# First stage of a decoder-layer kernel: conditioning sums gathered by a selection matrix, x transposed by token blocks, weight splits and parameter transposes reordered, separate waits for the next pool

## The chip, the cores and the metric

The kernel runs on one core of a Trainium2 chip. The time is device microseconds (us) of one execution on that core; the median over the runs is compared. Engines are called PE (TensorE, matmuls; its weight loads are shown apart as PEld), DVE (VectorE), ACT (ScalarE), POOL (GpSimd) and SP (SyncE, which here only issues DMAs).

## The reference

One inference step of a hybrid decoder layer: 512 prompt tokens and 8 sample tokens, width 1024. The part that the change touches is the start: the modulation from the conditioning vectors `c` (1 prompt, 8 samples), the first normalisation, and the first products with `w_in`.

```python
cs = jax.nn.silu(c.astype(F32))
mod = cs @ w_mod[l].astype(F32) + b_mod[l].astype(F32)        # 1024 -> 6*1024
sh1, sc1, g1, sh2, sc2, g2 = [m[:, None, :] for m in jnp.split(mod, 6, axis=-1)]
h = _rmsnorm(x, norm1_g[l]) * (1.0 + sc1) + sh1
u = h @ w_in[l].astype(F32)                                   # 1024 -> 8*1024
...                                                           # HGRN2, RG-LRU, two branches, w_out
x = (x.astype(F32) + g1 * (merged @ w_out[l].astype(F32))).astype(dt)
h2 = _rmsnorm(x, norm2_g[l]) * (1.0 + sc2) + sh2
ff = jnp.square(jax.nn.relu(h2 @ w_ff1[l].astype(F32))) @ w_ff2[l].astype(F32)
x = (x.astype(F32) + g2 * ff).astype(dt)
```

## The kernel before

All activations lie transposed: 128 features on the partitions, 520 tokens (512 + 8) along the row, in 8 blocks `k` of features. A large product (`products`, recorded at L111) takes fp32 data split into a high part in fp32r and a low part; each block `k` has 6 matmuls over halves of 260 columns: `whi` with h's high part, `whi` with h's low part, `wlo` with h's high part. Weights arrive by DMA in tiles `wst` of 512 KB; ACT casts the high part (`whi`), DVE subtracts it (`wlo`).

The first stage goes like this.

- SP issues the loads of c, x, the modulation weights `wm` (two tiles of 1 MB, scale and shift, for each pair of blocks k = 0, 2, 4, 6) and the first `wst` tiles. POOL issues the small parameter rows (`rb`, `rc`, `rd` among them).
- `transposed` turns x by PE transposes (L444) into the 4 banks of `pmm`, two blocks k at a time, and ACT and DVE copy the banks out (L445). `norm_x` and `normed` make the reciprocal root for each token; DVE multiplies (L459) all 8 blocks into `u`, which shares its memory with x as loaded (`xn`, so that name stands for u in the rows).
- `mod(k)` (L364) multiplies the conditioning, as a 32-column stationary operand `cT` of which 9 columns are used, by the two `wm` tiles. Four accumulations run side by side in the four 32-partition groups of one PSUM bank `ps` (j = 0 the first 256 columns, j = 1 the other 256): so four partial sums are left on partitions 0-31, 32-63, 64-95 and 96-127. ACT copies the bank to `modev` (L367).
- `mod_close` transposes modev in 4 pieces (L379), DVE adds the four partial sums with two reductions (L384), the bias (L387) and multiplies by the norm's gain (L391): `modT`.
- `affine_split(k)` makes h for blocks k and k+1: the sample columns on DVE (L468, L469), the high part on ACT (L472, with a cast of the sample columns, L476), the same in fp32 on DVE (L477) and the low part as the difference (L478).
- Between these, PE runs the products of the blocks that are ready, into two accumulators `acc` (the `pmm` banks), for the first two W_in tiles; `self.turn` chains the order on PE, `self.last_hi` and `self.split_last` that on ACT and DVE (`behind(a, b)`: a stands behind b).
- `parameters_in` transposes the small parameters (L224, rows rb, rc, rd, rd into `ps`) and DVE copies them (L225: pa, pb, pc). Then the pool `start`, which held the stage's memory, is closed and the pool `hg` opened in its place. The third W_in tile comes next, into the bank of the first sums once ACT has read them (L139, `e` and `X`).

`ps` has two PSUM banks (`pps`), used in turn; `pt` and `pb` have one each. What stands in a row on each engine is set by a scheduler within these chains; each engine then works its row in order. Later in the kernel, `mod_quarter` uses `mod` and `mod_close` for the other four parts, 8 times, each with one weight tile (so j = 0 alone, 512 columns).

The selection matrix of the change stands in the kernel already: `mdiag`, 128 x 4 x 32, is 1 where the partition modulo 32 equals the column:

```python
nc.vector.tensor_scalar(pi, pi, 31, None, OP.bitwise_and)
nc.vector.tensor_tensor(x, pi, ti, OP.bitwise_xor)
self.mdiag = sb.tile([128, NC, 32], F32, name="mdiag")
nc.vector.tensor_scalar(self.mdiag, x, 0.0, None, OP.is_equal)
```

Of the kernel before, what the change touches and what calls it, by code (L numbers as in the profile page):

```python
# [6 lines left out]
F32 = mybir.dt.float32  # L7
# [4 lines left out]
OP = mybir.AluOpType  # L12
# [4 lines left out]
L = 512  # L17
# [3 lines left out]
KO = D // 128  # L21
# [29 lines left out]
class Kernel:  # L51
# [304 lines left out]
    def mod(self, ws, ev, place):  # L356
# [3 lines left out]
        for j, w in enumerate(ws):  # L360
            n = w.shape[2]
            for k in range(KO):
                r = 32 * (k % 4)
                ins = nc.tensor.matmul(ps[r:r + 32, j * n:j * n + n], self.cT[:, k, :], w[:, k, :], start=k < 4, stop=k >= KO - 4)  # L364
                if self.ppt_free:
                    self.turn = self.behind(ins, self.turn) if self.turn else ins
        ins = nc.scalar.copy(ev, ps)  # L367
        if self.ppt_free and self.last_hi:
            self.behind(ins, self.last_hi)
        self.mod_open = ev, place  # L370

    def mod_close(self, after):
# [5 lines left out]
        for j in range(4):  # L378
            after = self.behind(nc.tensor.transpose(pt[:, j * 128:(j + 1) * 128], ev[:, j * 128:(j + 1) * 128], self.ident), after)  # L379
        out = self.modT.rearrange("p (a k) b -> p a k b", k=KO)[:, p0:p0 + np, k0:k0 + nk]  # L380
        bias = self.bmod.rearrange("p (a k) -> p a k", k=KO)[:, p0:p0 + np, k0:k0 + nk]
        got = pt.rearrange("p (a k j b) -> p a k b j", a=np, k=nk, b=32)[:, :, :, :NM]
        for a in range(np):
            ins = nc.vector.tensor_reduce(out[:, a], got[:, a], mybir.AxisListType.X, OP.add)  # L384
            if self.ppt_free and self.split_last:
                self.behind(ins, self.split_last)
        nc.vector.tensor_tensor(out, out, bias[..., None].to_broadcast([128, np, nk, NM]), OP.add)  # L387
# [43 lines left out]
    def transposed(self):  # L431
# [8 lines left out]
        for k in range(0, KO, 2):  # L440
            ps = self.pmm.tile([128, 2, 512], F32, name="mm")
            for j in range(2):
                for t in range(NC):
                    nc.tensor.transpose(ps[:, j, t * 128:(t + 1) * 128], self.xn[:, t, (k + j) * 128:(k + j + 1) * 128], self.ident)  # L444
                (nc.vector.tensor_copy if j else nc.scalar.copy)(self.x[k + j][:, :L], ps[:, j])  # L445

    def normed(self):
# [10 lines left out]
        for k in range(KO):  # L458
            nc.vector.tensor_tensor(self.u[:, k], self.x[k], rsb, OP.mult)  # L459

    def affine_split(self, k0):
# [7 lines left out]
        nc.vector.tensor_tensor(f[:, :, L:], f[:, :, L:], sh[:, :, 1:9], OP.add)  # L469
# [1111 lines left out]
```

## Time and profile before

| | us |
|---|---|
| median of 3 runs (lowest, highest) | 1018.2 (1018.13, 1018.38) |
| the profiled execution | 1018.91 |
| its span (first to last instruction) | 1017.1 |
| PE busy | 982.7 (97%) |
| DVE busy | 692.5 (68%) |
| ACT busy | 515.3 (51%) |
| the first stage, until the third W_in tile starts on PE | 52.42 |

The span is what the profiler sees from the first instruction to the last; the execution's time has some 1.8 us around it. A row of the timeline gives start, duration, engine, line and operation, output <- inputs with their shapes, how many instructions it groups, and in brackets the idle time of the engine before it with what released it. "PE busy" is modelled from pipelined matmuls. The granted clock is 1.00 at full speed.

### The profile page before, as it was taken

The numbers are of one execution on the slowest core, as the hardware profiler recorded it, in microseconds if no ns is written. First come the engines' busy times: TensorE is split into PE (matmuls) and PEld (weight loads), VectorE is DVE, ScalarE is ACT, GpSimd is POOL, SyncE is SP. The second block draws the span as 40 slices with busy tenths as digits, with TensorE's granted clock in tenths as the row PEclk, the third lists the DMA queues.
The fourth block names the chain that finished last, engine by engine and source line by source line (L and its number), as shares of the span: only waits on it lengthen the run. The fifth ranks groups of instructions, "written<-read, shape, count | busy, mean of one in ns | idle before, by whom it ended". The sixth has DMA issues, their size and how long they took to land.

```text
span 1017.1 us, 23291 instructions
## 1 busy us (share of the span) xinstructions
PE 982.7 (97%) x9585; PEld 955.5 (94%) x9585; DVE 692.5 (68%) x1543; ACT 515.3 (51%) x985; POOL 106.8 (10%) x193
## 2 busy tenths in 40 slices
PE   4999999999999999999999999999999999999995
PEld 3799999999999999999998999999999999999994
DVE  7678697687878868473233348667766776768775
ACT  5445753574565356351122234466556645646653
POOL 3000000000000000120000000022321331232040
PEclk9899999999999999999999999999999999999998
DMA  9884354344344434496656755322762483283242
GB/s 298 253 264 112 103 150 138 102 141 127 111 119 128 116 96 127 147 294 212 194 187 196 241 166 148 102 84 53 157 166 69 110 191 89 62 181 71 64 83 85
DMA packets 212572, 145.78 MB, mean 143 GB/s; under 512 B 6262, under 2 KB 196878, under 8 KB 212458
## 3 DMA queue, kind: packets, MB, share of 16 engines
q1 hardware_dynamic: 202562, 132.37, 43.9%
q0 software_dynamic: 9904, 11.92, 6.3%
q8 instruction: 75, 1.23, 0.5%
q14 instruction: 31, 0.25, 0.1%
HBM read 123.61 MB, written 13.39 MB: 135 GB/s over the span
## 4 chain that ended last, share of the span: by engine, by line
PE 88%; ACT 5%; DVE 4%; DMA 2%; issue 1%; SPq 0%; DVEq 0%; ACTq 0%
PE mm L111 63%; PE ps L1118 8%; PE pt L1118 4%; PE ps L364 2%; PE pb L1118 2%; PE pb L746 1%; PE ps L610 1%; DMA wst<-in_w_ff_dram 1%; DMA xn<-in_x_prompt_dram 1%; PE pt L677 1%; PE mm L1118 1%; PE pt L688 1%; PE pt L690 1%; ACT L794 1%; ACT L787 1%
## 5 line engine op out<-in xcount | busy, mean ns | idle before, releaser
L111 PE MATMUL mm<-h,whi 128*128 128x260 f32 (+1 forms) x3072 | 509.4, 285 | 1.9 <-ACT X L139 1.2
L111 PEld LDWEIGHTS mm<-h,whi 128*128 128x128 f32 x3072 | 426.9, 189 | 6.6 <-issue 4.1
L111 PE MATMUL mm<-h,wlo 128*128 128x260 f32 (+1 forms) x1536 | 313.1, 284 | 1.8 <-DVE wlo L80 1.4
L77 ACT CAST whi<-wst 128x1024 fp32r<-128x1024 f32 x166 | 173.6, 1049 | 218.0 <-PE mm L111 164.2
L80 DVE TENSOR_TENSOR wlo<-wst,whi 128x1024 fp32r<-128x1024 f32 x166 | 202.6, 1221 | 92.6 <-ACT whi L77 91.3
L111 PEld LDWEIGHTS mm<-h,wlo 128*128 128x128 f32 x1536 | 239.4, 189 | 2.3 <-DVE wlo L80 1.5
L111 PE MATMUL mm<-a,whi 128*128 128x260 f32 x512 | 83.0, 283 | 1.1 <-DVE rst L878 1.1
L111 PEld LDWEIGHTS mm<-a,whi 128*128 128x128 f32 x512 | 70.3, 188 | 2.1 <-issue 2.1
L111 PE MATMUL mm<-a,wlo 128*128 128x260 f32 x256 | 51.9, 283 | 0.0
L1214 DVE TENSOR_TENSOR f<-f 128x260 f32<-128x260 f32 x64 | 27.3, 427 | 28.9 <-ACT f L1209 28.2
L847 POOL DMA_DIRECT2D t<-oaT_d x8 | 4.3, 551 | 380.6 <-DVE wlo L80 374.7
L1203 ACT ACTIVATE ft<-ft,fsh 128x512 f32<-128x512 f32 (+2 forms) x36 | 24.0, 676 | 35.9 <-DVE ft L1200 35.9
L111 PE MATMUL mm<-b,whi 128*128 128x260 f32 x256 | 41.6, 284 | 0.0
L1206 POOL TENSOR_TENSOR ft<-ft,fsh 128x8 f32<-128x8 f32 x28 | 18.5, 659 | 216.9 <-DVE ft L1200 216.9
L111 PEld LDWEIGHTS mm<-a,wlo 128*128 128x128 f32 x256 | 39.4, 188 | 0.0
L111 PEld LDWEIGHTS mm<-b,whi 128*128 128x128 f32 x256 | 35.0, 188 | 2.5 <-ACT t L139 2.5
L596 DVE TENSOR_TENSOR Y<-Y,tb 128x512 f32<-128x512 f32 x40 | 27.5, 688 | 8.3 <-PE ps L610 7.2
L1248 POOL DMA_DIRECT2D ma<-snap x28 | 27.4, 979 | 35.4 <-issue 23.0
L863 DVE TENSOR_TENSOR t<-mm,t 128x520 f32<-128x520 f32 x8 | 5.6, 700 | 37.0 <-PE mm L111 37.0
L1230 POOL DMA_DIRECT2D ma<-snap x28 | 26.1, 932 | 43.8 <-DMA ma<-snap 27.2
L1209 ACT ACTIVATE f<-ft 128x520 f32<-128x520 f32 (+1 forms) x36 | 20.8, 587 | 14.9 <-POOL ft L1207 12.9
L555 ACT ACTIVATE st<-st,fkq 128x128 f32<-128x128 f32 x64 | 19.6, 389 | 16.4 <-DVE fkq L535 12.3
(488 smaller groups left out, 1815.0 us busy)
## 6 DMA issues: line engine op xcount, KB each, us to landing
wst<-in_w_in_dram SPq DMA_DIRECT2D x64, 512.0 KB, 4.3
wm<-in_w_mod_dram SPq DMA_DIRECT2D x8, 2048.0 KB, 7.9
wst<-in_w_ff_dram SPq DMA_DIRECT2D x64, 256.0 KB, 4.1
wst<-in_w_ff_dram SPq DMA_DIRECT2D x32, 512.0 KB, 4.0
wm<-in_w_mod_dram SPq DMA_DIRECT2D x8, 1024.0 KB, 10.7
st<-in_state_hgrn_dram SPq DMA_DIRECT2D x8, 512.0 KB, 4.9
vb<-vd SPq DMA_DIRECT2D x8, 512.0 KB, 4.0
out_dram<-st SPq DMA_DIRECT2D x8, 512.0 KB, 3.2
```

Of the source, the lines that this page charges most:

```text
L77: ins = self.nc.scalar.copy(hi, st)
L80: ins = self.nc.vector.tensor_tensor(lo, st, hi.bitcast(F32), OP.subtract)
L111: self.last_product = self.nc.tensor.matmul(ps[:, s, :c.stop - c.start], x, y[:, c], start=first and n == 0, stop=last and n == 2)
L364: ins = nc.tensor.matmul(ps[r:r + 32, j * n:j * n + n], self.cT[:, k, :], w[:, k, :], start=k < 4, stop=k >= KO - 4)
L555: nc.scalar.activation(st[:, b], st[:, b], AF.Copy, scale=fkq[:, 0, b:b + 1])
L596: made = nc.vector.tensor_tensor(view(Y, b, 0, 2 * b, n, b), view(X, b, 0, 2 * b, n, b), fac, OP.mult)
L1118: ins = self.nc.tensor.matmul(ps, x[:, w], y[:, f], start=j in (1, 7, 2) and k == 0 and n == 0, stop=k == 3 and n == 2, skip_group_check=True)
L1203: nc.scalar.activation(t[:, :p], t[:, :p], AF.Relu, bias=sh[:, 0:1])
L1209: nc.scalar.activation(f, self.two(self.ft)[:, a:a + n], AF.Square)
L1214: self.nc.vector.tensor_tensor(f[:, n], f[:, a], f[:, b], op)
L1230: nc.gpsimd.dma_start(x[1][:, b], v[:, :n], accum_op=OP.add)
L1248: nc.gpsimd.dma_start(x[t][:, a], s[p], accum_op=OP.add)
```

## The change

1. `mod` copies each half of the bank (j = 0, j = 1) with a copy of its own.
2. `mod_close` multiplies each 128-column piece of modev by the first 9 columns of `mdiag` instead of transposing it: the product adds the four partial sums and turns them at once, in 36 columns of `pt`. One DVE add with the bias (L385) takes the place of two reductions and an add.
3. `transposed` goes over token blocks first, and writes into 8 banks (the four of `pmm`, `pb`, both `ps`, `pt`); the 8 copies follow at the end, 5 on ACT and 3 on DVE.
4. `normed` no longer multiplies all 8 blocks at once: `scaled(n)` is called for blocks 0 to 3 before mod(0) and 4 to 7 before mod(2), each time behind the split of one weight tile. In `affine_split` the two blocks go one after the other on DVE.
5. `parameters_in` stands behind `affine_split(2)` instead of behind the last products.
6. The pool `hg` is opened with waits by tile: each of its tiles waits for what lay in its own memory, not for the whole pool `start`.

```diff
@@ -359,14 +359,15 @@
         ps = self.pps.tile([128, 512], F32, name="ps")
         for j, w in enumerate(ws):
             n = w.shape[2]
+            c = slice(j * n, j * n + n)
             for k in range(KO):
                 r = 32 * (k % 4)
-                ins = nc.tensor.matmul(ps[r:r + 32, j * n:j * n + n], self.cT[:, k, :], w[:, k, :], start=k < 4, stop=k >= KO - 4)
+                ins = nc.tensor.matmul(ps[r:r + 32, c], self.cT[:, k, :], w[:, k, :], start=k < 4, stop=k >= KO - 4)
                 if self.ppt_free:
                     self.turn = self.behind(ins, self.turn) if self.turn else ins
-        ins = nc.scalar.copy(ev, ps)
-        if self.ppt_free and self.last_hi:
-            self.behind(ins, self.last_hi)
+            ins = nc.scalar.copy(ev[:, c], ps[:, c])
+            if self.ppt_free and self.last_hi:
+                self.behind(ins, self.last_hi)
         self.mod_open = ev, place
 
     def mod_close(self, after):
@@ -376,15 +377,14 @@
         pool, name = (self.ppt, "pt") if self.ppt_free else (self.pps, "ps")
         pt = pool.tile([128, 512], F32, name=name)
         for j in range(4):
-            after = self.behind(nc.tensor.transpose(pt[:, j * 128:(j + 1) * 128], ev[:, j * 128:(j + 1) * 128], self.ident), after)
+            after = self.behind(nc.tensor.matmul(pt[:, j * NM:(j + 1) * NM], ev[:, j * 128:(j + 1) * 128], self.mdiag[:, 0, :NM],
+                                                 start=True, stop=True), after)
+        grid = lambda t: t.rearrange("p (a k) -> p a k", k=KO)[:, p0:p0 + np, k0:k0 + nk]
         out = self.modT.rearrange("p (a k) b -> p a k b", k=KO)[:, p0:p0 + np, k0:k0 + nk]
-        bias = self.bmod.rearrange("p (a k) -> p a k", k=KO)[:, p0:p0 + np, k0:k0 + nk]
-        got = pt.rearrange("p (a k j b) -> p a k b j", a=np, k=nk, b=32)[:, :, :, :NM]
-        for a in range(np):
-            ins = nc.vector.tensor_reduce(out[:, a], got[:, a], mybir.AxisListType.X, OP.add)
-            if self.ppt_free and self.split_last:
-                self.behind(ins, self.split_last)
-        nc.vector.tensor_tensor(out, out, bias[..., None].to_broadcast([128, np, nk, NM]), OP.add)
+        got = pt[:, :4 * NM].rearrange("p (a k b) -> p a k b", a=np, b=NM)
+        ins = nc.vector.tensor_tensor(out, got, grid(self.bmod)[..., None].to_broadcast([128, np, nk, NM]), OP.add)
+        if self.ppt_free and self.split_last:
+            self.behind(ins, self.split_last)
         for a in range(np):
             if p0 + a in (1, 4):
                 g = (self.n1g if p0 + a == 1 else self.n2g)[:, k0:k0 + nk]
@@ -437,12 +437,15 @@
             nc.tensor.transpose(ps[:, k * NB:(k + 1) * NB], self.xsn[:, k * 128:(k + 1) * 128], self.ident[:NB, :NB])
         for k in range(KO):
             nc.vector.tensor_copy(self.x[k][:, L:], ps[:, k * NB:(k + 1) * NB])
-        for k in range(0, KO, 2):
-            ps = self.pmm.tile([128, 2, 512], F32, name="mm")
-            for j in range(2):
-                for t in range(NC):
-                    nc.tensor.transpose(ps[:, j, t * 128:(t + 1) * 128], self.xn[:, t, (k + j) * 128:(k + j + 1) * 128], self.ident)
-                (nc.vector.tensor_copy if j else nc.scalar.copy)(self.x[k + j][:, :L], ps[:, j])
+        mm = [self.pmm.tile([128, 2, 512], F32, name="mm") for _ in range(2)]
+        banks = [m[:, j] for m in mm for j in range(2)]
+        banks += [pool.tile([128, 512], F32, name=name) for pool, name in
+                  ((self.ppb, "pb"), (self.pps, "ps"), (self.pps, "ps"), (self.ppt, "pt"))]
+        for t in range(NC):
+            for k, ps in enumerate(banks):
+                nc.tensor.transpose(ps[:, t * 128:(t + 1) * 128], self.xn[:, t, k * 128:(k + 1) * 128], self.ident)
+        for k, ps in enumerate(banks):
+            (nc.vector.tensor_copy if k in (1, 4, 6) else nc.scalar.copy)(self.x[k][:, :L], ps)
 
     def normed(self):
 
@@ -455,8 +458,12 @@
         rsb = self.c128[:, :T]
         nc.scalar.copy(rsb[:, :L], ps)
         nc.vector.tensor_copy(rsb[:, L:], p2[:, :NB])
-        for k in range(KO):
-            nc.vector.tensor_tensor(self.u[:, k], self.x[k], rsb, OP.mult)
+
+        def scaled(k):
+            ins = nc.vector.tensor_tensor(self.u[:, k], self.x[k], rsb, OP.mult)
+            if self.split_last:
+                self.behind(ins, self.split_last)
+        self.scaled = scaled
 
     def affine_split(self, k0):
 
@@ -466,7 +473,8 @@
         sc, sh = (self.modT[:, p * 8 + k0:p * 8 + k0 + 2] for p in (1, 0))
         u = self.u
         nc.vector.tensor_tensor(f[:, :, L:], u[:, ks, L:T], sc[:, :, 1:9], OP.mult)
-        nc.vector.tensor_tensor(f[:, :, L:], f[:, :, L:], sh[:, :, 1:9], OP.add)
+        sample = nc.vector.tensor_tensor(f[:, :, L:], f[:, :, L:], sh[:, :, 1:9], OP.add)
+        last = None
         for j in range(2):
             k = k0 + j
             ins = nc.scalar.activation(self.h_hi[:, k, :L], u[:, k, :L], AF.Identity, bias=sh[:, j, 0:1], scale=sc[:, j, 0:1])
@@ -474,7 +482,8 @@
                 self.behind(ins, self.last_hi)
             else:
                 self.last_hi = self.behind(nc.scalar.copy(self.h_hi[:, ks, L:T], f[:, :, L:]), ins)
-            nc.vector.tensor_scalar(f[:, j, :L], u[:, k, :L], sc[:, j, 0:1], sh[:, j, 0:1], OP.mult, OP.add)
+            mid = nc.vector.tensor_scalar(f[:, j, :L], u[:, k, :L], sc[:, j, 0:1], sh[:, j, 0:1], OP.mult, OP.add)
+            self.behind(mid, last or sample)
             last = nc.vector.tensor_tensor(self.h_lo[:, k, :T], f[:, j], self.h_hi[:, k, :T].bitcast(F32), OP.subtract)
         self.last_hi = ins
         return last
@@ -1443,9 +1452,9 @@
         for _, fn, *a in steps:
             fn(*a)
 
-    def open_pool(self, name, bufs):
+    def open_pool(self, name, bufs, **kw):
         self.scope = ExitStack()
-        return self.scope.enter_context(self.tc.tile_pool(name=name, bufs=bufs))
+        return self.scope.enter_context(self.tc.tile_pool(name=name, bufs=bufs, **kw))
 
     def close_pool(self):
         self.scope.close()
@@ -1469,8 +1478,10 @@
 
         def first_w(st):
             hi, lo = (self.start.tile([128, KO, 128], F32R, name=n, bufs=2) for n in ("whi", "wlo"))
-            self.behind(nc.scalar.copy(hi, st), ready)
-            nc.vector.tensor_tensor(lo, st, hi.bitcast(F32), OP.subtract)
+            self.behind(nc.scalar.copy(hi, st), self.last_hi or ready)
+            ins = nc.vector.tensor_tensor(lo, st, hi.bitcast(F32), OP.subtract)
+            if self.split_last:
+                self.behind(ins, self.split_last)
             return hi, lo
 
         pm, pl = self.parameters_mod(), self.parameters_bounds()
@@ -1492,9 +1503,9 @@
         self.normed()
         ready = nc.scalar.activation(self.act0, self.act0, AF.Sigmoid)
         self.behind(self.behind(ready, squares), self.exps)
-        first = [first_w(st) for st in staged]
         par = self.parameters()
         acc = [self.pmm.tile([128, 2, 512], F32, name="mm") for _ in range(2)]
+        first = []
 
         def products(todo):
             for j, k in todo:
@@ -1504,18 +1515,23 @@
 
         todo = []
         for k in range(0, KO, 2):
+            if k < 4:
+                first.append(first_w(staged[k // 2]))
+                for n in range(2 * k, 2 * k + 4):
+                    self.scaled(n)
             mod(k)
             products(todo[:1])
             self.turn = self.mod_close(self.turn)
             products(todo[1:])
             self.split_last = self.affine_split(k)
+            if k == 2:
+                self.parameters_in(*par)
             todo = [(j, k + n) for n in (0, 1) for j in (0, 1)]
         products(sorted(todo))
-        self.parameters_in(*par)
         self.decays()
         self.first = acc
         self.close_pool()
-        self.hg = self.open_pool("hg", 2)
+        self.hg = self.open_pool("hg", 2, reuse_waits="tile")
         self.ppt_free = False
         self.fkq = [self.hg.tile([128, 3, 32], F32, name=f"fkq{n}", bufs=1) for n in range(2)]
         for t in self.fkq:
```

The rows of the engines, in order, before and after, at the places where they differ most for what follows. `[waits ...]` names the engines or DMA queues whose semaphores the instruction waits for; line numbers of after are its own.

PE around mod(4) before, from the last products ahead of it (`h`, `whi`, `wlo`: operands of the products) to its close:

```order
L111 MATMUL mm<-h,wlo 128x260 x2
L364 MATMUL ps<-wm,cT 32x256 [waits DMAHW6_49]
L364 MATMUL ps<-wm,cT 32x256 x7
L364 MATMUL ps<-wm,cT 32x256 [waits DMAHW5_49]
L364 MATMUL ps<-wm,cT 32x256 x7
L111 MATMUL mm<-h,whi 128x260 [waits Activation_49] x2
```

The same place after:

```order
L111 MATMUL mm<-h,wlo 128x260 x2
L224 MATMUL ps<-ident,rb 128x57 [waits DMASW6_49,DMASW5_49,DMASW7_49,DMASW1_49,DMASW0_49]
L224 MATMUL ps<-ident,rc 128x64 [waits DMASW2_49,PE_49]
L224 MATMUL ps<-ident,rd 128x96 [waits DMASW3_49,DVE_49]
L224 MATMUL ps<-ident,rd 128x96 [waits DVE_49]
L365 MATMUL ps<-wm,cT 32x256 [waits DMAHW6_49,DVE_49]
L365 MATMUL ps<-wm,cT 32x256 x7
L365 MATMUL ps<-wm,cT 32x256 [waits DMAHW5_49,Activation_49]
L365 MATMUL ps<-wm,cT 32x256 x7
```

The four parameter transposes have moved in front of mod(4), whose first half waits for DVE as well as for its weights, and whose second half waits for ACT.

DVE after, from the end of affine_split(2) to the close of mod(4) (`ht` fp32 h, `h` its low part, `modT` the modulation):

```order
L485 TENSOR_SCALAR ht<-xn,modT 128x512
L487 TENSOR_TENSOR h<-ht,h 128x520
L485 TENSOR_SCALAR ht<-xn,modT 128x512
L487 TENSOR_TENSOR h<-ht,h 128x520
L225 COPY pa<-ps 128x57
L225 COPY pb<-ps 128x64
L225 COPY pc<-ps 128x96 x2
L385 TENSOR_TENSOR modT<-pt,pm 128x2x18
```

And before, the same step:

```order
L477 TENSOR_SCALAR ht<-xn,modT 128x512 x2
L469 TENSOR_TENSOR ht<-ht,modT 128x2x8
L478 TENSOR_TENSOR h<-ht,h 128x520 x2
L384 TENSOR_REDUCE modT<-pt 128x18 x2
L387 TENSOR_TENSOR modT<-modT,pm 128x2x18
```

The copies of the parameters now stand between the low part of h and the next modulation; before, pa and pb stood ahead of the last close and pc inside the last low part.

ACT after, around the second weight cast and the evacuation of mod(2):

```order
L480 ACTIVATE h<-xn,modT 128x512
L1481 CAST whi<-wst 128x1024
L368 COPY modev<-ps 128x256 x2
L480 ACTIVATE h<-xn,modT 128x512
L484 CAST h<-ht 128x2x8
```

The evacuation is two copies of 256 columns where one of 512 stood, and the second weight cast stands behind the high part of h(0) and h(1), where before both casts stood ahead of the first evacuation.

## Prediction

> **What bounds the kernel now.** I read the page's busy shares first, then a table of stretches of the first stage, then TensorE's waits, then the timeline of 15 to 53 us. Columns of the stretches: length, busy time of each engine (instructions), granted clock, DMA share, GB/s.
>
> ```profile
> PE 982.7 (97%) x9585; PEld 955.5 (94%) x9585; DVE 692.5 (68%) x1543; ACT 515.3 (51%) x985; POOL 106.8 (10%) x193
> ```
>
> ```profile
> 20.80:27.30 6.50, 0.78 (x8) 0.42 (x4) 6.50 (x15) 2.73 (x5) 0.00 (x0) 0.92 1.12 332
> 27.30:35.40 8.10, 8.06 (x60) 5.94 (x60) 4.80 (x18) 3.14 (x5) 0.00 (x0) 0.64 1.09 348
> 35.40:47.60 12.20, 12.20 (x127) 9.51 (x126) 7.50 (x25) 5.25 (x10) 0.00 (x0) 1.00 0.93 243
> 47.60:52.40 4.80, 2.96 (x23) 2.69 (x22) 4.40 (x11) 3.35 (x6) 0.76 (x3) 1.00 0.09 23
> 52.40:1017.00 964.60, 946.66 (x9286) 928.38 (x9286) 655.99 (x1412) 489.33 (x941) 98.13 (x170) 1.00 0.49 136
> ```
>
> TensorE (PE) is the bound: 98% busy after 52.4. So whatever the first stage gains or loses by its last product (the row at 52.42 below, where the third W_in tile starts) is carried to the end. Inside the stage, PE is idle for most of 20.8 to 27.3, while DMA runs at 332 GB/s, and is then full until 47.6.
>
> ```profile
> PE pt L379 <- ACT modev L367: 4.9, 1, 4.9
> PE ps L364 <- DVE ptmp L254: 0.8, 1, 0.8
> ```
>
> The 0.8 is not VectorE's: the program orders no such wait. mod(2) needs its two weight tiles. The wm issue at 19.5 (the tile behind) landed 10.7 us later, at 30.2; a 1 MB tile at 348 GB/s takes 3.0 us, so the tile ahead of it landed at about 27.2. The 4.9 is ScalarE's two weight casts standing before the first evacuation. Both lie ahead of that landing, which the change leaves where it is: SP's first loads keep their order.
>
> ```profile
> L353 SPq DMA_DIRECT2D wm<-in_w_mod_dram x1: 2792/2792/2792, 19.5 to 19.5; - x1
> DMA to landing us min/median/max: 10.7/10.7/10.7
> ```
>
> From there the timeline (start, duration, engine, line):
>
> ```profile
> 25.18 0.58 ACT L367 COPY modev<-ps 128x512 f32<-128x512 f32 x1
> 27.34 3.64 PE L364 MATMUL ps<-wm,cT 128*32 128x256 f32 x32 [0.82 <-DVE ptmp L254]
> 30.91 1.24 PE L111 MATMUL mm<-h,whi 128*128 128x260 f32 x4
> 32.38 0.95 PE L379 MATMUL pt<-ident,modev 128*128 128x128 f32 x4
> 33.37 0.37 DVE L384 TENSOR_REDUCE modT<-pt 128x18 f32<-128x72 f32 x2 [2.87 <-PE pt L379]
> 33.78 0.20 DVE L387 TENSOR_TENSOR modT<-modT,pm 128x36 f32<-128x36 f32 x1
> 35.42 1.93 PE L364 MATMUL ps<-wm,cT 128*32 128x256 f32 x32
> 35.67 1.42 DVE L478 TENSOR_TENSOR h<-ht,h 128x520 fp32r<-128x520 f32 x2 [0.27 <-ACT h L476]
> 37.47 0.59 ACT L367 COPY modev<-ps 128x512 f32<-128x512 f32 x1 [1.12 <-PE ps L364]
> 38.12 0.66 PE L379 MATMUL pt<-ident,modev 128*128 128x128 f32 x4
> 38.53 0.73 PE L111 MATMUL mm<-h,whi 128*128 128x260 f32 x4
> 40.88 1.93 PE L364 MATMUL ps<-wm,cT 128*32 128x256 f32 x32
> 43.06 0.27 PE L224 MATMUL ps<-ident,rb 57*128 57x57 f32 x1
> 43.26 0.63 PE L111 MATMUL mm<-h,whi 128*128 128x260 f32 x3
> 43.36 0.22 DVE L225 COPY pa<-ps 128x57 f32<-128x57 f32 x1 [0.84 <-PE ps L224]
> 44.26 0.66 PE L379 MATMUL pt<-ident,modev 128*128 128x128 f32 x4
> 44.95 0.37 DVE L384 TENSOR_REDUCE modT<-pt 128x18 f32<-128x72 f32 x2 [0.36 <-PE pt L379]
> 45.80 0.82 ACT L472 ACTIVATE h<-xn,modT 128x512 fp32r<-128x512 f32 x1 [2.28 <-DVE modT L391]
> 46.91 0.33 PE L224 MATMUL ps<-ident,rd 96*128 96x96 f32 x2
> 47.19 0.42 DVE L225 COPY pc<-ps 128x96 f32<-128x96 f32 x2 [0.22 <-PE ps L224]
> 47.53 1.30 DVE L478 TENSOR_TENSOR h<-ht,h 128x520 fp32r<-128x520 f32 x2
> 47.84 1.99 ACT L77 CAST whi<-wst 128x1024 fp32r<-128x1024 f32 x2
> 51.27 0.60 ACT L139 ACTIVATE e<-mm 128x520 f32<-128x520 f32 x1 [1.45 <-PE mm L111]
> 52.42 0.74 PE L111 MATMUL mm<-h,whi 128*128 128x260 f32 x4 [1.24 <-ACT X L139]
> ```
>
> The bracket is the idle time before, with its releaser. mod(2) takes 3.64 us and mod(4) 1.93 for the same 32 records, because the granted clock is half after the idle time, until about 33 (PE alone; length, busy, clock, DMA share, GB/s):
>
> ```profile
> 26.30:27.30 1.00, 0.22 (x2) 0.50 1.09 347
> 33.00:34.00 1.00, 1.00 (x10) 0.95 1.06 340
> ```
>
> **The change part by part.** The transposes of x by token block, the new order of scaled and the weight splits, and the earlier mod(0) all act before 27.2. I cost them at nothing: the landing covers them. If all of that were late by more than the 1.5 us by which mod(0)'s evacuation (25.2) precedes it, they would count; the new order takes a cast and a split away from before it, so I expect the reverse.
>
> *Halves of the modulation sums.* The program now copies the first half of the bank before PE may write the second, so PE waits in each mod. Rows for its size:
>
> ```profile
> L364 PE MATMUL ps<-wm,cT x128: 379/379/634, 18.9 to 42.4; 128*32 128x256 f32 x128
> L663 ACT COPY sev<-pt x8: 360/368/374, 85.5 to 397.3; 128x256 f32<-128x256 f32 x8
> ```
>
> At full clock a record is (1.93-0.38)/31 = 0.050 apart. The first 16 end at 15x0.05+0.38 = 1.13; ScalarE starts 0.12 later (37.35 to 37.47), copies for 0.37, and I allow 0.05 for PE to resume: 1.67 against 0.80 now, a wait of 0.87. At half clock: spacing (3.64-0.63)/31 = 0.097, so 15x0.097+0.63+0.54 = 2.63 against 1.55, a wait of 1.08. The last copy is 0.22 shorter (0.37 for 0.59), which the close gets back when it waits for it. In the trace of before, PE never waits in the middle of a mod. Bounds: 0.5 (copy and handovers alone) to 1.1 each. By the Trainium skill ("PSUM — Partial Sum Buffer", PSUM bank collisions raise a hardware error), two engines must be kept apart by bank and quadrant, not by address, so disjoint columns don't help here. That rule speaks against this part: without the wait the sum would be some 2.8 lower, with it the sum stands; no run here shows an overlap.
>
> *Closes.* Four products with the selection matrix replace four transposes (0.41 on PE: 38.12 to the next product at 38.53), and one VectorE add replaces two reduces and an add. An fp32 product is two records. The nearest row below, eight small records from 3.3 to 4.1, gives 0.11 apart at the low clock, thus at most 8x0.11 = 0.88; at the least 0.41 as now. I take 0.5, since only 9 columns move. VectorE saves 0.41 (33.37 to 33.78) in each chain. In the later stage there are 8 more closes, 32 transposes: 0 to 8x0.47 = 3.8 us, taken as 0.2: PE is full there, so nothing hides them, but the records that replace the transposes are shorter, and at full clock two of them may go by in the time of one.
>
> ```profile
> L379 PE MATMUL ps<-ident,modev x32: 270/272/273, 468.1 to 601.5; 128*128 128x128 f32 x32
> L339 PE MATMUL pt<-ident,c x8: 241/250/250, 3.3 to 4.1; 9*128 9x9 f32 x8
> ```
>
> *parameters_in moved.* Its four transposes (rb, rc, rd, rd) now stand before mod(4) on PE, its copies (pa, pb, pc) on VectorE behind the low part of h(3). The two "ps" banks alternate: rd waits for the copy of pa, mod(4) for that of pc. So mod(4), which today starts 0.25 us before that low part does, must wait for its end and for three copies. All of mod(4), its products and its evacuation are queued behind that. It leaves the tail: 0.20 twice on PE (43.06, 44.05), rd and pc (0.42).
>
> *Separate waits of the next pool.* The activations of the first sums (51.27) wait for PE's last products, 1.45 us. After the change they wait only for their own sums, finished two products (1.44) earlier; the 1.24 gap mostly goes. What is late next is ScalarE: two casts of 1.99 stand before them.
>
> *Sum* (us, before in brackets). First product 30.91+1.08 = 32.0. Close(2) 33.4 (32.38); its add at 34.2; the low part of h(3) ends 3.31 later (3.72-0.41) at 37.5 (37.09). Then pa 0.22, rd 0.3, pc 0.25 and handovers: mod(4) at 38.3 (35.42). PE has nothing from about 36.2 on: a new wait of 2.1. Close(4): 2.70+0.87-0.22 later, 41.65 (38.12). mod(6) 44.5 (40.88). Close(6): 3.38+0.65-0.40 later, 48.1 (44.26): +3.85. Tail: before 8.16 from close to 52.42. Now the add stands 0.75 behind the close, h's high part 0.41 on (0.20, 0.18 and handovers) at 1.16 (before 1.54), its second piece ends near 3.1, two casts to 5.1, two activations to 6.2; PE's ten closing products also end near 6. So 54.3, tail 6.2: -1.95. Net +1.9, later closes +0.2: 2.1 on a profiled execution of 1018.9 (span 1017.1), which is 0.7 above the median of 1018.2. Where terms have room (the low bound of the waits, a quick close) the sum comes to +1.0. I take +1.9 on the median: 1020.1. Such a kernel tells about 0.2% (2.0 us) from no change.
>
> **Rivals.**
> 1. *Full clock at 27 us.* The new transposes run without pauses and ScalarE frees mod(0) sooner, but PE must still sit idle from about 21 to 27. Were the clock full: first product 27.34+1.86+0.87 = 30.1, mod(4) near 35.7 (+0.3), close(6) +1.2, end -0.7, later closes +0.2: 1017.7. Against it: 4.9 idle before, clock half afterwards.
> 2. *The new idle time drops the clock again* (ends slower). Half clock lasted from 26.3 to about 33 in the trace. If the 2.1 us without work before mod(4), with the stall inside mod(2), suffice, mod(4) to close(4) and its products run at half rate for up to 6.8 us: about +2.7, 1022.8. It decides if that gap exceeds what the chip forgives; the gap of 1.24 at 51.2 was forgiven (clock 1.00), that of 4.9 not. The Trainium skill ("TensorE: Matmul & The Clock Gate", Part 1) puts the drop at an idle window of about 3.4 us; by that this rival would not come, and the trace so far agrees.
> 3. *Later closes cost in full*: +3.8 instead of 0.2, 1023.7. For: fp32 products take two passes. Against: the small records were that far apart only at the low clock.
> 4. *The stage is worth more than the sum*: the separate waits let the loads and the memsets of the next pool start sooner, and some of the 17.9 us that PE idles after 52.4 goes: -3, 1015.5. Against: that idle time is spread over hundreds of us. If the wait inside the mods were not there after all, 2.8 would come off the sum, 1017.3.
>
> **How the numbers follow.** Sum as worked out: 0.56, itself from +0.2 to +3.2, half of it beyond 2.0. Rival 1: 0.20 (0.08 faster by over 0.2%, 0.12 within). Rival 2: 0.10, rival 3: 0.05, both slower. Rival 4: 0.09, faster. So faster 0.17, same 0.40 (0.28+0.12), slower 0.43 (0.28+0.15). The range takes in rival 1 with its spread and rival 2: 1016.3 to 1022.9, leaving out rivals 3 and 4 and a little of rival 1's low end.
>
> **What would show it.** In the trace of after: a pause of 0.8 to 1.1 in each mod between its 16th and 17th record, ended by ScalarE's copy; PE idle about 2 us before mod(4), ended by VectorE's pc; mod(4) near 38.3, close(6) near 48.1, the third tile near 54.3 with less than 0.5 idle before it; a clock of half only around 27 to 33. Wrong, if mod(2) starts well before 27.2 or takes under 2.5 us, if mod(4) starts before 37, or if the time from there to the end differs by over 1 us from before.

## The result, and the profile after

The changed kernel takes 1028.26 us (median of 4, 1027.18 to 1030.32), before 1018.28 in the same comparison: ratio 1.0101, interval 1.0083 to 1.0118. It is 10 us slower; I had said 1020.1, with 1022.9 as the upper end. The profiled execution took 1028.51 us, its span is 1026.7, 9.6 more than before.

The stretches of the changed kernel's first stage, as before: length, busy time of PE, granted clock, DMA share, GB/s (PE alone).

```profile
12.60:14.90 2.30, 0.00 (x0) 1.00 1.09 314
15.00:27.30 12.30, 7.51 (x47) 0.50 1.12 332
27.30:38.80 11.50, 10.92 (x64) 0.50 1.10 343
39.00:50.00 11.00, 9.45 (x105) 1.00 0.63 152
```

The clock is half from 15.0 to 38.9, where it was half from 26.3 to 33.1 before. The early start costs nothing, since mod(2) waits for its weights until 27.2 anyway (the bracket of its row below names VectorE, but the last packet of these weights landed at 27.21 in both kernels). The late end does: from 27.3 to 38.8 PE is nearly full, at half rate.

The timeline of the changed kernel, its rows in the order of those shown of before:

```profile
27.34 1.93 PE L365 MATMUL ps<-wm,cT 128*32 128x256 f32 x16 [2.65 <-DVE ht L485]
29.39 0.37 ACT L368 COPY modev<-ps 128x256 f32<-128x256 f32 x1 [1.65 <-PE ps L365]
29.81 1.94 PE L365 MATMUL ps<-wm,cT 128*32 128x256 f32 x16 [0.54 <-ACT modev L368]
31.68 1.24 PE L111 MATMUL mm<-h,whi 128*128 128x260 f32 x4
33.14 1.72 PE L380 MATMUL pt<-mdiag,modev 128*128 128x9 f32 x8
34.71 1.21 PE L111 MATMUL mm<-h,whi 128*128 128x260 f32 x4
38.89 0.27 PE L224 MATMUL ps<-ident,rb 57*128 57x57 f32 x1
39.47 0.44 PE L224 MATMUL ps<-ident,rd 96*128 96x96 f32 x2 [0.24 <-DVE pa L225]
40.12 1.07 PE L365 MATMUL ps<-wm,cT 128*32 128x256 f32 x16 [0.22 <-DVE pc L225]
41.74 1.07 PE L365 MATMUL ps<-wm,cT 128*32 128x256 f32 x16 [0.55 <-ACT modev L368]
43.56 0.95 PE L380 MATMUL pt<-mdiag,modev 128*128 128x9 f32 x8
44.37 0.73 PE L111 MATMUL mm<-h,whi 128*128 128x260 f32 x4
50.15 0.95 PE L380 MATMUL pt<-mdiag,modev 128*128 128x9 f32 x8
56.57 0.71 PE L111 MATMUL mm<-h,whi 128*128 128x260 f32 x4
63.10 2.46 ACT L564 ACTIVATE st<-st,fkq 128x128 f32<-128x128 f32 x8 [5.73 <-DMA st<-in_state_hgrn_dram]
```

mod(2) starts at 27.34 as before. ScalarE's copy splits it with a pause of 0.54. Its close takes 1.57 to the next product (33.14 to 34.71) at half clock and 0.81 at full (43.56 to 44.37), against 0.41 for the transposes at 38.12. The third weight tile starts at 56.57, 4.15 later than before.

After that, two more losses. The waits of PE in the changed kernel (total, times, longest) have a new line:

```profile
PE mm L111 <- DVE e L534: 1.9, 1, 1.9
```

It lies near 69 us: ScalarE stands idle 5.73 for the state's load (row 63.10). An evacuation by ScalarE (`e`, at 67.37) is queued behind its state steps, and VectorE's L534, which frees PE's next accumulator, comes behind that. PE was 4.15 us late at the third tile (56.57), and behind this wait it is 6.2 late (70.27, where before the same place in its row is at 64.06). And the eight later closes (instructions, shortest/median/longest duration in ns, first and last start):

```profile
L380 PEld LDWEIGHTS ps<-mdiag,modev x64: 187/192/192, 474.3 to 611.4; 128*128 128x128 f32 x64
L380 PE MATMUL ps<-mdiag,modev x64: 171/257/257, 474.4 to 611.4; 128*128 128x9 f32 x64
```

From the first to the last of them 137.0 us pass, 133.4 before: 3.6 more, 0.45 for each of the eight. The three losses, 4.15, 2.05 and 3.6, add up to 9.8; the span is 9.6 longer, so some 0.2 is gained elsewhere.

### The profile page after: what moved, and what is told of

Its sections match the earlier page's. It is cut to its first block, busy times and chain, and to the rows that moved or that the text cites. A ratio compares the mean times of both kernels' runs of the same rounds, so it can differ in the third digit from the quotient of the medians.

```text
span 1026.7 us, 23383 instructions
## 1 busy us (share of the span) xinstructions
PE 993.0 (97%) x9633; PEld 965.1 (94%) x9633; DVE 689.6 (67%) x1526; ACT 516.1 (50%) x990; POOL 106.9 (10%) x193
## 4 chain that ended last, share of the span: by engine, by line
PE 86%; ACT 5%; DVE 4%; DMA 2%; issue 1%; SPq 0%; DVEq 0%; ACTq 0%
PE mm L111 61%; PE ps L1127 8%; PE pt L1127 4%; PE ps L365 2%; PE pb L1127 2%; PE pb L755 1%; PE ps L619 1%; PE pt L686 1%; PE mm L1127 1%; DVE wlo L80 1%; DMA wst<-in_w_ff_dram 1%; PE pt L697 1%; DMA xn<-in_x_prompt_dram 1%; DMA st<-in_state_hgrn_dram 1%; DVE st L565 1%
## 5 line engine op out<-in xcount | busy, mean ns | idle before, releaser
L1223 DVE TENSOR_TENSOR f<-f 128x260 f32<-128x260 f32 x64 | 27.3, 427 | 29.0 <-ACT f L1218 28.3
L365 PE MATMUL ps<-wm,cT 128*32 128x256 f32 (+1 forms) x256 | 27.4, 554 | 6.0 <-ACT modev L368 3.1
L872 DVE TENSOR_TENSOR t<-mm,t 128x520 f32<-128x520 f32 x8 | 5.6, 700 | 38.3 <-PE mm L111 38.3
```

The costliest lines, as they stand in the source:

```text
L365: ins = nc.tensor.matmul(ps[r:r + 32, c], self.cT[:, k, :], w[:, k, :], start=k < 4, stop=k >= KO - 4)
L1223: self.nc.vector.tensor_tensor(f[:, n], f[:, a], f[:, b], op)
```

## The experiments

The runs are told in three groups: one part of the change taken out, parts alone, and what is left. The edits alone differ; no kernel leaves out work that the outputs need, unless it is said. Ratios are to the kernel before, run on the same chip beside it.

**One part out of the changed kernel.** The first takes out the closing products (the two reductions and the add on VectorE come back with the transposes):

```diff
-            after = self.behind(nc.tensor.matmul(pt[:, j * NM:(j + 1) * NM], ev[:, ...], self.mdiag[:, 0, :NM], start=True, stop=True), after)
+            after = self.behind(nc.tensor.transpose(pt[:, j * 128:(j + 1) * 128], ev[:, ...], self.ident), after)
```

> The changed kernel with the closes as before: four transposes, two reductions and an add. Theory A (the closing products cost twice a transpose, and in the first stage their few columns also keep the clock at half): the eight later closes give back 8 x 0.44 = 3.5 us, the four of the stage 0.9 + 3 x 0.44 = 2.2, and the clock is back at full by 35.5 instead of 38.9, another 1.7: 1028.3 - 7.4 = 1021 us. Rival B (the pause in the middle of a mod keeps the clock down, the closes cost only their own time): half clock still until 38.9, 1028.3 - 5.5 = 1022.8. Rival C (closes cost nothing, as I took in the prediction): 1028 within 1.

Measured: 1023.27 us (ratio 1.0053, 1.0038 to 1.0068), 5.0 less. Rival C is out. The size fits B better than A, but the clock did something that neither expected (granted clock in three stretches of this run):

```profile
33.30:40.00 6.70, 4.36 (x45) 1.00 1.13 328
40.10:43.50 3.40, 3.40 (x25) 0.50 1.20 289
43.60:50.00 6.40, 5.85 (x65) 1.00 0.19 45
```

It was back at 33.3, earlier than A said. PE then waited for VectorE's copies ahead of mod(4) and for ScalarE's copy in its middle, 2.3 us idle out of 6.7 in all, and the clock fell again for 3.4 us.

The second takes out the halves:

```diff
-            ins = nc.scalar.copy(ev[:, c], ps[:, c])      # inside the loop over j
+        ins = nc.scalar.copy(ev, ps)                       # behind it
```

> The changed kernel with one evacuation of the whole bank, so no pause inside a mod. Theory A: three pauses on the path of about 0.55 to 0.9 each go, the clock stays half until 38.9 because of the closing product at 33 to 35: -2 us, 1026.3. Rival B (the pause keeps the clock down): the clock is full from about 35.5 or earlier, -2 - 1.7 to -3: about 1024. If the halves cost nothing: 1028.

Measured: 1023.56 (1.0069, 1.0047 to 1.0090), 4.7 less, spread 1022.52 to 1027.52. In the profiled execution, the fastest of the four, the clock was back at 30.4; where it came back in the others is not known. The size fits rival B.

The third puts the parameters back:

```diff
-            if k == 2:
-                self.parameters_in(*par)
...
         products(sorted(todo))
+        self.parameters_in(*par)
```

> The changed kernel with the parameter transposes back behind the last products. Theory A: they cost little where they stand now, since PE is slow at half clock until 38.9 and mod(4) waits for them only 0.5 us; moved back they interrupt the tail by 0.4 to 1: no change within 1 us (1027.5 to 1029). Rival D (my prediction's step: mod(4) waits 2 us because of them): -2, 1026.

Measured: 1024.98 (1.0069, 1.0048 to 1.0091), 3.3 less, with executions from 1022.73 to 1027.18. Theory A fails here: the parameters do cost, although PE waits for them only 0.46 us in the profile of the changed kernel. In this run's profile, again that of its fastest execution, the clock was back at 30.7, with halves and closing products in place.

The fourth:

```diff
-        self.hg = self.open_pool("hg", 2, reuse_waits="tile")
+        self.hg = self.open_pool("hg", 2)
```

> The changed kernel with the next pool waiting for the whole first pool, as before. If the 1.9 us that PE waits near 68 us (behind ScalarE, which waits for the state's load until 63.1) comes from the new order of loads, that wait goes, and the 1.2 us gap ahead of the third weight tile comes back: 1028.3 - 1.9 + 1.2 = 1027.6. If that wait comes from somewhere else, only the gap comes back: 1029.5.

Measured: 1027.01 (1.0090, 1.0075 to 1.0105), 1.25 less; the first forecast was 1027.6. The separate waits lose a little here: in this run's profile PE's wait near 69 us is gone, the gap of 1.24 ahead of the third tile is back, and the clock is half from 15.0 to 38.9 as in the changed kernel.

The four differences are between medians of two comparisons, in which the kernel before stood at 1018.28 and at 1017.70. Each against the kernel before beside it, they are 4.4, 4.1, 2.7 and 0.7, together 11.9 where 10.0 were lost; with executions of one kernel up to 5 us apart, that excess is not clear of noise. That the first three parts bear on the clock is seen in the profiles alone: without them it was back at 33.3, 30.4 and 30.7, in the changed kernel at 38.9.

**One part alone on the kernel before.** The closing products:

> The kernel before with the closing products alone. Theory A: eight later closes 8 x 0.45 = +3.6 us, three closes of the stage on the path +0.44 each minus 0.41 on VectorE at the last one, and if a window of the clock that holds a close at half rate doesn't count as busy, half clock lasts one step of 3.4 us longer (+1.7): +4.5 to +6.5, 1022 to 1024. Theory of my prediction (0.2 for the later closes, 0.5 for each in the stage): +0.5.

Measured: 1021.82 (1.0038, 1.0023 to 1.0053), +3.9, less than expected. The eight later closes are 3.6 of it: from the first to the last of them it takes 3.6 longer than before. In this profile nothing is lost ahead of them: the first later close starts at 467.5, 0.6 earlier than before's. But that holds for this execution. Its clock was half from 23.7 to 30.5, where the profile of before has 26.3 to 33.1, although the two kernels do the same up to 25 us; the run with the tile waits alone has 23.4 to 30.2. So when the clock comes back differs by some 3 us from one execution to another, and the earlier return hides here what the three closes of the stage cost. The edit is the change's own `mod_close`; so is `mod` in the next.

> The kernel before with the two half evacuations alone. Theory A: a pause on PE of 0.55 (full clock) to 0.6 in mods 2, 4 and 6, some 1.1 longer at half clock for the first, less 0.2 per shorter last copy: +1.5 to +2.5, and up to 1.7 to 3.4 more in executions where the pause keeps a window of the clock from counting as busy; 1019.5 to 1022, with a wider spread than before's 1.4 us. If the pauses are hidden: 1018.

Measured: 1023.21 (1.0051, 1.0034 to 1.0068), +5.3, from 1021.3 to 1024.91. More than expected, and for a reason that I had not seen: without the new order of the weight splits, both casts stand ahead of ScalarE's copy of mod(0)'s first half, and PE waits for that copy with mod(0)'s second half. In this run's timeline:

```profile
24.37 1.05 ACT L1473 CAST whi<-wst 128x1024 fp32r<-128x1024 f32 x1 [2.15 <-DMA wst<-in_w_in_dram]
25.32 0.37 ACT L368 COPY modev<-ps 128x256 f32<-128x256 f32 x1
25.74 1.93 PE L365 MATMUL ps<-wm,cT 128*32 128x256 f32 x16 [5.52 <-ACT modev L368]
28.78 1.94 PE L365 MATMUL ps<-wm,cT 128*32 128x256 f32 x16
```

mod(2) starts at 28.78, 1.4 late. The clock is half from 21.2 to 38.3 in this profile, with the transposing closes and the parameters at their old place, and the third tile starts at 57.24, 4.8 later than before. So this run can't be read as the price of the halves in the changed kernel, but it shows that the clock can come back as late without the closing products.

The tile waits:

> The kernel before with waits by tile in the next pool alone. Theory A: the gap of 1.24 us ahead of the third weight tile goes (about -1), but the state's load is issued behind the same last products and now shares the DMA with a weight load, ScalarE's first state step is 1.5 to 2 us later against PE, and PE waits for that near 63: +0.5 to +1 net, 1018.3 to 1019. If nothing is given back: 1016.9.

Measured: 1017.86, ratio 1.0001 (0.9991 to 1.0010): even. The gap of 1.24 is gone, and PE waits 0.9 for an evacuation (`e`, L525) further on.

Then a test of the clock itself, on the kernel before: work that nobody reads, in PE's idle time (`warm` is a tile of the bank `pb`).

```diff
+        def fill(n):
+            for i in range(n):
+                c = slice(i % 4 * 128, i % 4 * 128 + 128)
+                self.turn = self.behind(nc.tensor.transpose(warm[:, c], self.ident, self.ident), self.turn)
...
             mod(k)
+            if k == 0: fill(40)
...
             self.turn = self.mod_close(self.turn)
+            if k == 0: fill(8)
```

> The kernel before with 48 transposes of the identity into an unread bank in PE's idle time, 40 between mod(0) and its close and 8 behind the close. If the half clock from 26.3 to 33.1 is due to PE's idle time from 20.9 to 27.3, it stays full, mod(2) takes 1.93 instead of 3.64, mod(4) then waits for its weights at 33.2 (35.42 before) and mod(6) for its own at 38.9 (40.88 before): -1.9 us, about 1016. If idle time in front of mod(2) isn't what sets the clock: no change, or +0.3.

Measured: 1017.38, ratio 0.9995 (0.9986 to 1.0005): no difference that can be told. But the clock did what was expected of it (length, PE busy, granted clock):

```profile
20.00:27.90 7.90, 5.79 (x52) 1.00 1.12 335
27.90:33.80 5.90, 5.71 (x61) 1.00 1.09 348
```

Its timeline at mod(6):

```profile
39.85 1.93 PE L364 MATMUL ps<-wm,cT 128*32 128x256 f32 x32 [0.49 <-DMA wm<-in_w_mod_dram]
```

So PE's idle time ahead of mod(2) goes with the half clock: the kernel before and its variants with one part alone (closing products, halves, tile waits) all have a spell of half clock of 6.8 us or more there in their profiles, and the filled kernel has none. The gain is cut off at mod(6), which now waits for its own weights, in this execution until 39.85 (40.88 before, forecast 38.9).

**What is left without them.** Both the closing products and the halves out of the changed kernel:

> The changed kernel without the closing products and without the halves (x by token blocks, the split order, the parameters before mod(4) and the tile waits stay). Theory A (those two parts are the loss): at most the pause before mod(4) of 1 to 1.5 us is left, with the gap before the third tile gone and the later wait of 1 to 1.5 come: 1018 to 1020. Rival E (the parts that stay cost as much): 1022 or more.

Measured: 1020.63 (1.0027, 1.0017 to 1.0036), between the two forecasts. Then the parameters put back too:

> Only x by token blocks, the split order and the tile waits are kept. Theory A: mod(2) still waits for its weights at 27.2, so nothing is gained ahead of it, and the stage is as before or up to 1 us shorter; the tile waits come out even: 1017 to 1018.5. Rival D (the parameters before mod(4) cost nothing): the same as the run without matrix and halves.

Measured: 1017.69, ratio 0.9996 (0.9987 to 1.0005). So the token blocks, the split order and the tile waits together make no difference that can be told, and the place of the parameters costs the difference, 2.9 us. The timeline of the run without closing products and halves shows how:

```profile
34.53 0.23 PE L224 MATMUL ps<-ident,rc 64*128 64x64 f32 x1
36.07 0.21 DVE L225 COPY pa<-ps 128x57 f32<-128x57 f32 x1
36.34 0.43 PE L224 MATMUL ps<-ident,rd 96*128 96x96 f32 x2 [1.58 <-DVE pa L225]
36.99 2.68 PE L364 MATMUL ps<-wm,cT 128*32 128x256 f32 x32 [0.22 <-DVE pc L225]
```

PE waits 1.8 for VectorE's copies (1.58 and 0.22), and mod(4), 1.93 at full clock, takes 2.68: the clock falls at 38.1 in the middle of it, until 41.5.

Filling the idle time of the changed kernel, with 8 and 5 transposes, shows what stood behind its half clock:

> The changed kernel with 13 transposes of the identity into an unread bank, 8 between mod(0) and its close and 5 behind the close, so that PE works through from 21 to 27. If it is the clock that makes the stage cost more than the pauses and the closes themselves, it is full again by 28.6 or 32 instead of 38.9, and the time falls by 2 to 4 us to 1024 to 1026. If the loss is in the pauses and closes alone: 1028 or a little more.

Measured: 1029.41 (1.0113, 1.0098 to 1.0128); not faster. Its stretches:

```profile
27.00:33.70 6.70, 5.70 (x41) 0.50 1.09 348
33.80:40.50 6.70, 4.88 (x48) 1.00 1.14 325
40.60:44.00 3.40, 3.40 (x26) 0.51 1.21 292
71.30:74.60 3.30, 3.30 (x17) 0.50 0.69 187
```

Its timeline ahead of mod(4):

```profile
38.02 0.43 PE L224 MATMUL ps<-ident,rd 96*128 96x96 f32 x2 [1.06 <-DVE pa L225]
38.67 1.07 PE L365 MATMUL ps<-wm,cT 128*32 128x256 f32 x16 [0.22 <-DVE pc L225]
```

The clock was back 5 us sooner (33.8 for 38.9). PE was through sooner, ran into the wait for the parameters' copies, and the clock fell again at 40.6; mod(6) starts at 46.82, no earlier than in the changed kernel (46.71). A further spell of half clock, from 71.3 to 74.7, follows PE's wait of 1.76 for `e` and takes 1.5 more (the first later close starts at 475.9 for 474.4). In these profiles, either PE is late at half clock and hardly waits for the copies, or it is early, waits, and the clock falls. That fits with the parameters looking almost free in the profile of the changed kernel (0.46 us) while taking them out gave about 3.

Why a closing product costs what it does was asked with one record for each instead of two (operands in fp32r: `modev`, and a copy of ten columns of `mdiag`), on the kernel before; modev is rounded by it.

```diff
-            ... matmul(pt[:, j * NM:(j + 1) * NM], ev[:, ...], self.mdiag[:, 0, :NM], ...)
+            ... matmul(pt[:, j * 10:(j + 1) * 10], ev[:, ...], self.mdiag_r, ...)
```

> The kernel before with closing products whose operands are fp32r (modev and a 10-column selection), so that each is one record and not two; modev is rounded to fp32r. If a closing product is dear because fp32 loads its 128x128 weights twice, the eight later closes cost what four transposes cost (0.44 us), the 3.6 us vanish, and the time is that of before: 1017.5 to 1018.5. If few columns make it dear, it stays at 1021 or more.

Measured: 1017.18, ratio 1.0000 (0.9990 to 1.0009). The later closes of this run:

```profile
L381 PEld LDWEIGHTS ps<-mdiag_r,modev x32: 187/190/192, 465.7 to 599.2; 128*128 128x128 f32 x32
```

32 weight loads and not 64, each as long as with fp32 operands (190 ns for 192), and first to last 133.5 us as with the transposes. Four of these records take 0.36 on PE to the next product (465.82 to 466.18), the four transposes 0.35 (468.11 to 468.46) and the eight records in fp32 0.80 (474.43 to 475.23): some 0.1 each, with 10, 128 or 9 columns, and with weight loads of 190, 139 or 192 ns. So a closing product costs by its number of records; fewer columns did not make one cheaper. What sets the 0.1 of a record is not shown.

Last, a version that keeps what did no harm, with the parameters ahead of mod(0), where PE and VectorE have time:

```diff
         todo = []
+        self.parameters_in(*par)
+        self.split_last = self.copied          # the last of its copies: scaled() and the splits stand behind it
```

> x by token blocks, the split order and the tile waits kept, and the parameter transposes and copies placed ahead of mod(0), where PE and VectorE have time. If the place before mod(4) was what cost 2.9 us, they cost nothing here, and the tail has 0.4 us on PE and 0.4 on VectorE less: 1016.5 to 1017.5. If they delay mod(0) and its close beyond the weights' landing at 27.2: 1018 or more.

Measured: 1017.15, ratio 0.9994 (0.9984 to 1.0003). With 6 and 20 filling transposes (e14 in the expectation behind it):

> The same with 26 transposes of the identity, 6 behind mod(0) and 20 behind its close, to keep the clock up to mod(2). If the half clock around 27 to 31 is all that is left above the weights' landing: mod(4) waits for its weights at 33.2 and mod(6) at 38.9, 1 us less than without: about 1016. If the clock falls nonetheless: as without.

Measured: 1017.33, ratio 0.9997 (0.9988 to 1.0006): no better than without. In this run's profile the third tile starts 3.8 us sooner than before (48.67), and PE then waits 2.3 for `e`, behind ScalarE, which stands 6.06 for the state's load. The same kernel with the old pool waits:

> The kernel of e14 with the next pool waiting for the whole first pool, as before. The state's load is issued behind the last product either way, and ScalarE's state steps and the evacuation behind them follow from its landing. If that chain swallows what the tile waits give (2.4 us in e14), the gap of 1.24 ahead of the third tile comes back and the wait near 62 shrinks by as much: the same time as e14 within 0.5, 1017. If the tile waits cost more than they give, 1015.5 to 1016.5.

Measured: 1016.76, ratio 0.9990 (0.9981 to 0.9999), the only run whose interval lies below 1, by a hair: 1 us. Its 1.24 gap is back and the wait for `e` is down from 2.3 to 0.3:

```profile
PE ps L364 <- DMA wm<-in_w_mod_dram: 2.2, 2, 1.2
PE mm L111 <- ACT X L139: 1.2, 1, 1.2
PE mm L111 <- DVE e L534: 0.3, 1, 0.3
```

So taking that gap away gains little by itself: the state's load starts behind the last product, and the chain from its landing through ScalarE's state steps to the next evacuation ends at nearly the same time (the state steps start at 55.44 here and at 55.53 with the tile waits; the first later close at 466.9 and 467.0).

## Why the prediction was wrong

- **What bounds the stage: right.** mod(2) started at 27.34 in both, and all that was gained ahead of it (mod(0) at 17.55) gave nothing. The run that keeps only the transposes, the splits with the earlier mod(0) and the tile waits shows no difference (0.9996).
- **The pause inside a mod: right.** From first to second half I had 2.63 at half clock and 1.67 at full; measured 2.47 and 1.62. First product 31.68, forecast 32.0.
- **The closes: the step that failed first.** I bounded a close by 0.41 and 0.88 and took 0.5, because only 9 columns move. It is 0.81 at full clock, near the upper bound, and 1.57 at half. The term for the eight later closes, 0.2, measured 3.6. My rival 3 had that price (3.8), at a chance of 0.05. I argued against it that small records were 0.11 apart only at the low clock, and that shorter records might go by two in the time of one. At full clock eight of them take 0.81, so they are 0.10 apart there too, and the run in fp32r shows that the number of records is what is paid.
- **The clock: the second failed step.** I let it come back at 33 as before. It came back at 38.9 in the changed kernel, and in three runs with the parameters ahead of mod(4) where it came back early (33.3, 33.8, 31.3) it fell again for 3.4 us in mod(4); in a fourth, the whole evacuation, it did not in the profiled execution. Rival 2 said that the clock falls again there, with 2.1 us of idle time (measured 1.8 to 2.3 in the 6.7 us ahead) and +2.7; I gave it 0.10. It is true of those three runs. In the profile of the changed kernel itself the clock had not come back by then, which no rival said. The argument against rival 2 was wrong: the gap of 1.24 at 51.2 was forgiven, 4.9 was not, and I put 2.1 with the former. The idle window of about 3.4 us, on which the prediction leaned against rival 2, was not needed: the longest single wait in these runs was 1.6. And the return at 33 that I carried over was that of one execution; others of the same stage have it at 30.2 to 30.5.
- **mod(4).** Forecast 38.3, measured 40.12, and its wait was 0.46 and not 2.1, because PE itself was late at half clock. With the clock up, mod(4) starts at 38.67 with waits of 1.06 and 0.22 (the filled kernel) and at 38.23 with 1.57 and 0.22 (without the closing products): the start was right for the clock that I had assumed, the wait somewhat too long.
- **The tail: right, then taken back.** From the last close to the third tile 6.42 (50.15 to 56.57), forecast 6.2, before 8.16. I stopped there. The prediction had written that whatever the stage gains by 52.42 is carried to the end; the chain from the state's load ends 12 us further on and took 2.05 back. That step failed too; with the old pool waits this wait is not there.
- **The sum.** +1.9 by the third tile, measured +4.15; later closes +0.2, measured 3.6; +2.05 not foreseen. The direction was the likeliest of my three, by 0.43 to 0.40, and the size was off by a factor of five. The price of the closes stood among the rivals, and so did a loss by the clock, though in another form. I priced each alone as unlikely and had no term for both together.

What stays open is at which share of idle time the clock falls, and what brings it back. Counted in steps of 3.41 us from the clock's own edges, a stretch with 1.7 us of idle time made it fall in one run, one with 1.3 did not, and in the profile of before one with 2.0 idle between 19.5 and 22.9 did not either, so idle time alone isn't the measure. Nor is it for the return: behind a stretch with 0.54 us of idle time in mod(2) the clock came back in the run with the parameters last (at 30.7), and in the changed kernel (at 32.1) it did not. Whether the closing products themselves keep the clock down (the clock stayed half over the stretch 32.0 to 35.5, in which PE was never idle and eight closing records ran) was not tried apart. The changed kernel's executions lie 3 us apart. Those of the kernel before lay 0.25 apart in the first comparison, but up to 4.2 in a later one with 25 executions. A return that comes a step of 3.4 us earlier or later would do this, but only the profiled executions show where it came.

## What to carry to other kernels

Before an instruction is replaced by a "smaller" one, count the records behind it: here, in fp32, a matmul of 9 columns cost as much PE time as two 128-column transposes, and eight closes of four such matmuls in a full part of the kernel cost 3.6 us that no list of waits shows. A wait can look short in a profile only because the engine that waits is itself late at half clock, as the 0.46 ahead of mod(4); price it again for the clock that the change is meant to restore. And follow a gain past the point where it is made, to the next load that starts at that point: it may be the real end of the chain.

## What the runs showed of the hardware

- The half-clock spells have lengths of 3.4 (40.1 to 43.5), 6.8 (26.3 to 33.1) and 23.9 us (15.0 to 38.9): 1, 2 and 7 steps of 3.41. The Trainium skill ("TensorE: Matmul & The Clock Gate", Part 1) has a free-running window of 3413 ns; these spells agree with it.
- 48 transposes of the identity in fp32, 0.11 us apart, kept the clock at 1.00 from 20.0 to 27.9, where PE had been idle for most of the time and the clock had fallen. The Trainium skill ("TensorE: Matmul & The Clock Gate", Part 4) says that the full clock does not engage for transpose mode, which does not count as busy in the same way; in this run such transposes were enough to keep it.
- Pauses of 1.8 to 2.3 us in all, within the 6.7 us ahead, went with a fall to half clock for 3.4 us, in three kernels.
